# Level matmuls of a gated recurrence placed one unit later, with the operands of the first level made in the slot they have now

## The chip, the cores and the metric

One core of a Trainium2 chip runs the whole program. The metric is the device time of one execution in microseconds (us), as the median of several runs; lower is better. The engines of the core are TensorE (PE, matmuls), VectorE (DVE, elementwise work), ScalarE (ACT, functions and copies), GpSimd (POOL, elementwise work beside them) and SyncE (SP, which issues most transfers). Each works through its own queue in order and waits for the others by semaphores.

## The reference

A decoder layer over 512 tokens of width 1024. One input projection feeds three branches; the first of them is a gated linear recurrence with four heads of key and value width 128, and only its core bears on this change:

```python
def step(state, inp):
    qc, kc, vc, lc = inp
    b = jnp.cumsum(lc, axis=2)
    diff = b[:, :, :, None, :] - b[:, :, None, :, :]
    decay = jnp.where(causal, jnp.exp(jnp.where(causal, diff, 0.0)), 0.0)
    attn = jnp.einsum('bhtk,bhsk,bhtsk->bhts', qc, kc, decay)
    o = (jnp.einsum('bhts,bhsv->bhtv', attn, vc)
         + jnp.einsum('bhtk,bhkv->bhtv', qc * jnp.exp(b), state))
    b_last = b[:, :, -1:, :]
    new_state = (jnp.exp(b_last[:, :, 0, :])[..., None] * state
                 + jnp.einsum('bhsk,bhsv->bhkv', kc * jnp.exp(b_last - b), vc))
    return new_state, o
...
h = rms_norm(x, g_mix[l])
p = h @ w_in[l]
q, fp, iv, go, bg, cg, xc, u, v, gates = jnp.split(p, offsets, axis=-1)
o_a = hgrn2_mix(q, fp, iv, go, lbs[l], g_hgrn_out[l])
o_b = short_conv_mix(bg, cg, xc, w_conv[l])
o_c = spatial_gating_mix(u, v, sg_ln_g[l], sg_ln_b[l], w_sg[l], b_sg[l])
...
merged = jnp.sum(gate * y, axis=2)
x = x + merged @ w_o[l]
h2 = rms_norm(x, g_ffn[l])
x = x + jnp.square(jax.nn.relu(h2 @ w_ff1[l])) @ w_ff2[l]
```

A final RMS norm follows.

## The kernel before

The program is a list of **units**. A unit is one block of big matmuls on TensorE: typically a projection of 128 output columns for all 512 tokens, which is 24 matmuls of 128x512 (each product is made of three, L98 to L100, from a high and a low half of both operands). Units 0 to 3 project the forget gate, 4 to 7 the queries, 8 to 11 the values of the spatial branch, 12 to 15 its `u`, 16 to 19 the output gate, 20 to 31 the short convolution (`cg`, `xc`, `bg` in turn), and from 32 on come the merge gates and the branch outputs, then the output projection and the MLP.

Around each unit there are hooks, written into two tables by `at(...)`. What stands in `pre` for unit *i* (slot *i*) is recorded before the unit's matmuls, what stands in `post` behind them. Every engine keeps the recorded order, so a slot decides where in each engine's queue an instruction stands. Within a slot the order is: ScalarE's part of a weight split (`split_hi`, the high half `wh`), the evaluation of the unit before, the `take` hooks, VectorE's part of the weight split (`split_lo`, the low half `wl`), and then the other hooks in the order in which they were put down. A unit's weights are split two slots ahead of it.

The recurrence goes through seven levels. A level *l* builds the part of the causal attention matrix between neighbouring blocks of 2^l tokens. Heads are handled in two pairs, heads 0 and 1 (`p` = 0), and heads 2 and 3 (`p` = 1). For each pair and level there are three steps:
- `prep` (L281): ScalarE exponentials (L289, or L292 and L293), GpSimd additions that update the sums for the next level (L79, POOL), and VectorE multiplications that make the operands. At level 0 VectorE also does one reciprocal per head (L307), so that a head costs a reciprocal and four multiplications there.
- `level` (L318): four small matmuls per head (L326, 128x128) into a PSUM bank. The profile shows two records for each.
- `take` (L328): a predicated copy on VectorE (L332), which moves the wanted part of that bank into the attention tile and with that empties the bank.

Behind the levels come the states between the blocks of 128 tokens (`far_prep`, `far_turn`, `far_state` L362, `far_scan` L368 and L370), the outputs (`mix`, L379 and L381), a norm over the head (`mix_norm`, `mix_scale`) and a transpose (`head_turn`, L402, `head_out`). The constant `S0` is the slot at which the first level of the first pair is prepared; all other slots of the recurrence count from it. PSUM has eight banks, taken from one pool (`acc`, L72).

These lines set the slots:

```python
s0 = S0 + 2 * l + p
at(post, s0 + 1, level, pairs[p], l)
at(pre, s0 + 2, take, pairs[p], l)
at(pre, s0, prep, pairs[p], l)
```

Of the kernel before, what the change touches and what calls it, by code (L numbers as in the profile page):

```python
# [25 lines left out]
LB_FLOOR = 1e-30  # L26
LOG_SHIFT = 50
WARM = 8
S0 = 9
LN2 = 0.6931471805599453  # L30

V_GMIX, V_LB, V_GH, V_CONV, V_GFFN, V_GFIN, V_LG, V_LB2, V_N = 0, 8, 12, 16, 28, 36, 44, 48, 52
# [4 lines left out]
def trunk_kernel(ctx: ExitStack, tc, xT, x_t, w_f, w_t, w_bc, w_a, w_o, w_1, w_2, vecs, rows, gfin, w_sg, cst, lmask, out):  # L37
# [141 lines left out]
    pre, post = {}, {}  # L179

    def at(table, slot, fn, *a):
        table.setdefault(slot, []).append((fn, a))
# [397 lines left out]
    pairs = ((0, 1), (2, 3))  # L580
    for p in range(2):
        for l in range(7):
            s0 = S0 + 2 * l + p
            at(post, s0 + 1, level, pairs[p], l)
            at(pre, s0 + 2, take, pairs[p], l)
            at(pre, s0, prep, pairs[p], l)
        s0 = S0 + 14 + p
        at(pre, s0, far_prep, pairs[p])
        at(post, s0 + 1, far_turn, pairs[p])
        at(pre, s0 + 2, far_take, pairs[p])  # L590
        at(post, s0 + 2, far_state, pairs[p])
        at(pre, s0 + 3, far_scan, pairs[p])
        s0 += 3
        at(post, s0, mix, pairs[p])
        at(pre, s0 + 1, mix_norm, pairs[p])
        at(pre, s0 + 1, mix_scale, pairs[p])
        at(post, s0 + 2, head_turn, pairs[p])
        at(pre, s0 + 3, head_out, pairs[p])
# [569 lines left out]
```

## Time and profile before

| | |
|---|---|
| median of 3 runs | 835.8 us (835.66 to 835.86) |
| profiled execution, own time | 836.52 us |
| its span, first to last instruction | 834.7 us |
| PE busy | 819.6 us (98%) |
| DVE busy | 542.2 us (65%) |
| ACT busy | 346.0 us (41%) |
| POOL busy | 155.6 us (19%) |
| mean granted TensorE clock | 0.992 |

The profile is one execution. Busy times are shares of its span; time outside the span is start and end of the program. A busy TensorE can run at full clock (1.00, 2.4 GHz) or at half of it (1.2 GHz), which the granted clock shows as a mean over a stretch. Times in the rows below are us from the start of the span.

### The profile page before, as it was taken

To read this page: it belongs to the slowest core of one execution; us is meant where nothing else is said; L and a number is where in the kernel's file an instruction comes from. 1 tells how busy PE (TensorE), PEld (TensorE's weight loads), DVE (VectorE), ACT (ScalarE), POOL (GpSimd) and SP (SyncE) were. 2 spreads that over 40 slices of the span, in tenths; PEclk is the share of its full clock that TensorE was granted. 3 is DMA by queue.
4 is the path that set the end of the run, shared out by engine and by line. 5 is a ranking of instruction groups with operands and counts; after the bars stand their busy time and mean duration, and the time that the engine had idled before them with its cause. 6 is when DMAs were issued, how large, how long until landed. Compare 5 with 4: busy or idle time off the path is not lost.

```text
span 834.7 us, 9871 instructions
## 1 busy us (share of the span) xinstructions
PE 819.6 (98%) x3798; PEld 683.8 (82%) x3798; DVE 542.2 (65%) x706; ACT 346.0 (41%) x519; POOL 155.6 (19%) x187
## 2 busy tenths in 40 slices
PE   8999899999999999999999999999999999999995
PEld 7888688888988888888888888888888888888884
DVE  7556989878574455444554435868677777777763
ACT  7567365454433233222322434543434343434432
POOL 4312654562111000000000011202020202020000
PEclk9999899999999999999999999999999999999998
DMA  8322221212122322223235236657484838383502
GB/s 306 126 80 73 76 90 67 72 51 89 64 76 89 113 89 89 90 100 114 89 102 213 86 121 197 197 132 209 119 217 112 225 102 245 88 248 86 166 0 102
DMA packets 30431, 102.45 MB, mean 123 GB/s; under 512 B 3504, under 2 KB 3888, under 8 KB 30384
## 3 DMA queue, kind: packets, MB, share of 16 engines
q1 hardware_dynamic: 20736, 67.45, 23.3%
q0 software_dynamic: 9360, 34.08, 16.6%
q8 instruction: 30, 0.49, 0.2%
q10 hardware_dynamic: 288, 0.29, 0.1%
q14 instruction: 17, 0.14, 0.0%
HBM read 99.71 MB, written 2.10 MB: 122 GB/s over the span
## 4 chain that ended last, share of the span: by engine, by line
PE 95%; DVE 2%; issue 2%; DMA 1%; ACT 0%; SPq 0%; POOLq 0%; POOL 0%; DVEq 0%
PE acc L98 29%; PE acc L99 29%; PE acc L100 29%; PE acc L326 3%; PE acc L1058 1%; DVE h L79 1%; DVE wl L79 1%; DMA raw<-w_t 1%; PE acc L478 0%; PE acc L379 0%; PE acc L641 0%; DVE h L307 0%; PE acc L381 0%; PE acc L362 0%; PE acc L402 0%
## 5 line engine op out<-in xcount | busy, mean ns | idle before, releaser
L98 PE MATMUL acc<-x,wh 128*128 128x512 f32 x672 | 263.6, 392 | 0.0
L100 PE MATMUL acc<-x,wl 128*128 128x512 f32 x672 | 261.6, 389 | 0.0
L99 PE MATMUL acc<-x,wh 128*128 128x512 f32 x672 | 261.5, 389 | 0.0
L972 ACT ACTIVATE wh<-raw 128x1024 fp32r<-128x1024 f32 (+1 forms) x114 | 116.6, 1025 | 246.7 <-PE acc L99 143.5
L79 DVE TENSOR_TENSOR wl<-raw,wh 128x1024 fp32r<-128x1024 f32 (+1 forms) x120 | 153.2, 1278 | 44.1 <-ACT wh L972 43.8
L100 PEld LDWEIGHTS acc<-x,wl 128*128 128x128 f32 x672 | 126.1, 188 | 26.4
L98 PEld LDWEIGHTS acc<-x,wh 128*128 128x128 f32 x672 | 126.2, 188 | 25.8 <-issue 0.2
L99 PEld LDWEIGHTS acc<-x,wh 128*128 128x128 f32 x672 | 126.2, 188 | 25.7 <-issue 0.2
L79 DVE TENSOR_TENSOR h<-h,acc 128x512 f32<-128x512 f32 x118 | 75.6, 681 | 11.1 <-PE acc L100 11.0
L79 DVE TENSOR_TENSOR z<-z,z 128x1024 fp32r<-128x1024 f32 x51 | 61.6, 1218 | 32.1 <-ACT z L766 32.1
L692 ACT ACTIVATE h<-tmp 128x512 f32<-128x512 f32 x32 | 20.2, 633 | 125.6 <-DVE tmp L691 125.6
L766 ACT ACTIVATE z<-z 128x1024 fp32r<-128x1024 f32 x51 | 53.1, 1051 | 45.0 <-PE acc L100 28.2
L99 PE MATMUL acc<-z,h 128*128 128x512 f32 x184 | 71.6, 389 | 0.0
L100 PE MATMUL acc<-z,h 128*128 128x512 f32 x184 | 71.6, 389 | 0.0
L98 PE MATMUL acc<-z,h 128*128 128x512 f32 x184 | 71.6, 389 | 0.0
L79 DVE TENSOR_TENSOR h<-h,h 128x256 f32<-128x256 f32 (+4 forms) x89 | 66.4, 750 | 7.6 <-ACT h L745 3.6
L79 DVE TENSOR_TENSOR tmp<-acc,rb 128x512 f32<-128x512 f32 x28 | 19.3, 691 | 79.0 <-PE acc L100 79.0
L762 POOL DMA_DIRECT2D z<-w x28 | 24.5, 873 | 231.7 <-DVE z L79 195.6
L79 POOL TENSOR_TENSOR tmp<-tmp,tmp 128x512 f32<-128x512 f32 x15 | 20.0, 1332 | 198.0 <-DVE tmp L79 185.0
L691 DVE SCALAR_TENSOR_TENSOR tmp<-acc,rb 128x512 f32<-128x512 f32 x32 | 22.0, 686 | 30.9 <-PE acc L100 30.9
L100 PEld LDWEIGHTS acc<-z,h 128*128 128x128 f32 x184 | 34.5, 188 | 7.3
L98 PEld LDWEIGHTS acc<-z,h 128*128 128x128 f32 x184 | 34.5, 188 | 7.2
(187 smaller groups left out, 1071.7 us busy)
## 6 DMA issues: line engine op xcount, KB each, us to landing
z<-w POOLq DMA_DIRECT2D x65, 512.0 KB, 6.3
raw<-w_f SPq DMA_DIRECT2D x52, 512.0 KB, 3.3
raw<-w SPq DMA_DIRECT2D x34, 512.0 KB, 5.2
raw<-w_bc SPq DMA_DIRECT2D x8, 512.0 KB, 3.3
raw<-w_o SPq DMA_DIRECT2D x8, 512.0 KB, 3.3
raw<-w_t SPq DMA_DIRECT2D x4, 512.0 KB, 3.2
raw<-w_a SPq DMA_DIRECT2D x8, 256.0 KB, 2.6
h<-x_t SPq DMA_DIRECT2D x4, 512.0 KB, 7.0
```

The lines of the kernel that those rows point to most:

```text
L79: return e.tensor_tensor(out=o, in0=a, in1=b, op=op)
L98: pe.matmul(o, lh, rh, start=start, stop=False, skip_group_check=more)
L99: pe.matmul(o, lh, rl, start=False, stop=False, skip_group_check=more)
L100: pe.matmul(o, ll, rh, start=False, stop=stop, skip_group_check=more)
L326: pe.matmul(ps[:, cs(b)], kl[:, cs(b)], qk[:, cs(b)], start=True, stop=True)
L691: dve.scalar_tensor_tensor(out=t, in0=part["f", i], scalar=0.0, in1=part["r2b"], op0=ALU.max, op1=ALU.mult)
L692: act.activation(hf["a" if r < 2 else "b"][:, cs(r % 2, S)], t, AF.Square)
L762: pool.dma_start(wr[n, g], w_2[g, src[0], src[1]], accum_op=ALU.add)
L766: act.activation(hi, wr[src, g], AF.Copy)
L972: act.activation(hi[:, :n], raws[i][:, :n], AF.Copy)
L1058: pe.matmul(a4[t], lh, rh, start=j == 0 and rnd == 0, stop=j == KD - 1 and rnd == 2)
```

## The change

`S0` goes from 9 to 10, which puts every step of the recurrence one slot later, and the first level's `prep` alone is held at the slot that it has now.

```diff
@@ -26,7 +26,7 @@
 LOG_SHIFT = 50
 WARM = 8
-S0 = 9
+S0 = 10
 LN2 = 0.6931471805599453
@@ -583,7 +583,7 @@
             s0 = S0 + 2 * l + p
             at(post, s0 + 1, level, pairs[p], l)
             at(pre, s0 + 2, take, pairs[p], l)
-            at(pre, s0, prep, pairs[p], l)
+            at(pre, s0 - (l == 0), prep, pairs[p], l)
```

On TensorE, at the end of unit 10, the kernel before has level 0 of heads 0 and 1 (`acc_844` and `acc_849` are their banks, `h_394` and `h_395` head 0's operands, `h_434` and `h_435` head 1's) ahead of unit 11 (weights `wh_752`, `wl_753`).

```order
L100 MATMUL acc_727<-wh_705,x_243 128x512
L326 MATMUL acc_844<-h_394,h_395 128x128 x4
L326 MATMUL acc_849<-h_434,h_435 128x128 x4
L98 MATMUL acc_724<-wh_752,x_263 128x512
L99 MATMUL acc_724<-wl_753,x_263 128x512
```

In the changed kernel the same two rows stand behind unit 11 and ahead of unit 12 (`wh_798`, `wl_799`).

```order
L98 MATMUL acc_727<-wh_752,x_292 128x512
L99 MATMUL acc_727<-wl_753,x_292 128x512
L100 MATMUL acc_727<-wh_752,x_293 128x512
L326 MATMUL acc_874<-h_394,h_395 128x128 x4
L326 MATMUL acc_879<-h_434,h_435 128x128 x4
L98 MATMUL acc_910<-x_141,wh_798 128x512
```

The matmuls of one level have moved past the 24 of one unit. A unit later, in the changed kernel, level 0 of heads 2 and 3 (`h_474` to `h_516`) stands behind unit 12, and unit 13 (`wh_844`) follows; the waits are shown here.

```order
L326 MATMUL acc_935<-h_474,h_475 128x128 [waits DVE_49]
L326 MATMUL acc_935<-h_474,h_475 128x128 x3
L326 MATMUL acc_940<-h_515,h_516 128x128 [waits DVE_49,Activation_49]
L326 MATMUL acc_940<-h_515,h_516 128x128 x3
L98 MATMUL acc_967<-x_141,wh_844 128x512 [waits DVE_49]
```

The wait of unit 13's first matmul for VectorE (`DVE_49`) is, in the built program, for the predicated copy of `acc_874`, whose bank it takes over; in the kernel before it is unit 12 that waits for the copy of `acc_844`.

On VectorE, behind the operands of head 3 (`h_515`, `h_516`), the difference is this; `wl_845` is the low half of unit 13's weights, `wl_855` the same tile in the kernel before, and `wl_885` that of unit 14.

```order
 L79 TENSOR_TENSOR h_516<-z_514,h_515 128x256 x2
-L332 COPY_PREDICATED h_397<-lm,acc_844 128x512
-L332 COPY_PREDICATED h_437<-lm,acc_849 128x512
-L79 TENSOR_TENSOR wl_855<-raw_772,wh_854 128x1024
+L79 TENSOR_TENSOR wl_845<-raw_772,wh_844 128x1024
+L332 COPY_PREDICATED h_397<-lm,acc_874 128x512
+L332 COPY_PREDICATED h_437<-lm,acc_879 128x512
+L79 TENSOR_TENSOR wl_885<-raw_818,wh_884 128x1024
 L79 TENSOR_TENSOR h_395<-h_394,z_393 128x128x2
```

The two copies of level 0 now stand behind one weight split, and the operands of level 1 behind two. All VectorE rows ahead of these keep their order.

On ScalarE the exponentials of level 1 of heads 0 and 1 stand in the kernel before directly behind `wh_854`; in the changed kernel a further weight split and the four copies of unit 11's evaluation (L426) stand in front of them.

```order
L972 ACTIVATE wh_884<-raw_818 128x1024
L426 ACTIVATE z_887<-acc_724,rstd 128x512
L426 ACTIVATE z_887<-acc_725,rstd 128x512
L426 ACTIVATE z_890<-acc_726,rstd 128x512
L426 ACTIVATE z_890<-acc_727,rstd 128x512
L292 ACTIVATE h_394<-h_396 128x128x2
L293 ACTIVATE h_394<-z_393 128x128x2
```

GpSimd's additions of level 1 wait for these exponentials; their own order does not change there.

## Rows read from the trace of the kernel before

**Rows 1.** The page's busy times: engine, us, share of the span, instructions.

```profile
PE 819.6 (98%) x3798; PEld 683.8 (82%) x3798; DVE 542.2 (65%) x706; ACT 346.0 (41%) x519; POOL 155.6 (19%) x187
```

**Rows 2.** Waits of TensorE: total us, times, longest us.

```profile
PE acc L326 <- DVE h L79: 3.8, 2, 2.8
```

**Rows 3.** Stretches: us, busy PE, PEld, DVE, ACT, POOL, PEclk, DMA share, GB/s.

```profile
88.39:91.73 3.34, 2.48 (x11) 1.71 (x10) 3.34 (x6) 0.82 (x1) 3.18 (x5) 1.00 0.32 128
90.90:97.90 7.00, 3.21 (x17) 3.04 (x18) 7.00 (x9) 2.55 (x5) 5.18 (x7) 0.71 0.00 0
112.00:819.00 707.00, 707.00 (x3302) 591.43 (x3302) 459.52 (x593) 274.62 (x404) 114.73 (x139) 1.00 0.41 122
```

**Rows 4.** TensorE's timeline at level 0: start, duration, instruction, [idle before].

```profile
90.49 0.39 PE L100 MATMUL acc<-wh,x 128*128 128x512 f32 x1
91.86 1.16 PE L326 MATMUL acc<-h,h 128*128 128x128 f32 x8 [0.99 <-DVE h L79]
95.85 2.05 PE L326 MATMUL acc<-h,h 128*128 128x128 f32 x8 [2.83 <-DVE h L79]
```

**Rows 5.** Chain of work that ended last: start, us on the chain.

```profile
97.90 0.43 PE acc L98
...
100.86 0.23 PE acc L99
...
104.75 1.78 PE acc L326 x16
...
111.99 1.78 PE acc L326 x16
```

**Rows 6.** VectorE's timeline from 88 to 103 us.

```profile
88.39 1.67 DVE L79 TENSOR_TENSOR h<-h,h 128x256 f32<-128x256 f32 x2
...
91.73 1.74 DVE L307 RECIPROCAL h<-h 128x256 f32<-128x256 f32 x1
93.39 1.64 DVE L79 TENSOR_TENSOR h<-h,h 128x256 f32<-128x256 f32 x2
...
95.63 1.21 DVE L79 TENSOR_TENSOR wl<-raw,wh 128x1024 fp32r<-128x1024 f32 x1
96.76 1.74 DVE L307 RECIPROCAL h<-h 128x256 f32<-128x256 f32 x1
98.43 0.68 DVE L79 TENSOR_TENSOR h<-h,h 128x256 f32<-128x256 f32 x2
...
99.70 1.74 DVE L307 RECIPROCAL h<-h 128x256 f32<-128x256 f32 x1
...
102.64 1.34 DVE L332 COPY_PREDICATED h<-lm,acc 128x512 f32<-128x512 uint8 x2
```

**Rows 7.** GpSimd's timeline, additions of level 1, heads 0 and 1.

```profile
93.17 0.84 POOL L79 TENSOR_TENSOR h<-h,z 128x256 f32<-128x256 f32 x1
...
96.34 1.20 POOL L79 TENSOR_TENSOR h<-h,z 128x256 f32<-128x256 f32 x1 [1.59 <-ACT h L292]
97.62 0.61 POOL L79 TENSOR_TENSOR z<-z 128x256 f32<-128x256 f32 x1
```

**Rows 8.** ScalarE's timeline, level 1 behind unit 11's end.

```profile
108.03 0.45 ACT L292 ACTIVATE h<-h 128x256 f32<-128x256 f32 x1
```

**Rows 9.** Timelines of VectorE and TensorE at the outputs, 215 to 234 us.

```profile
215.92 1.05 PE L379 MATMUL acc<-z,h 128*128 128x128 f32 x8
...
225.84 1.05 PE L379 MATMUL acc<-z,h 128*128 128x128 f32 x8
226.73 0.83 PE L381 MATMUL acc<-h 128*128 128x128 f32 x6
...
222.31 0.28 DVE L368 COPY h<-acc 128x128 f32<-128x128 f32 x1
...
223.28 0.28 DVE L368 COPY h<-acc 128x128 f32<-128x128 f32 x1
...
233.53 0.69 DVE L79 TENSOR_TENSOR h<-acc,rr 128x512 f32<-128x512 f32 x1 [0.28 <-POOL tmp L499]
```

## The prediction before the run

> **What bounds the kernel now.** I read the table of busy times first: TensorE is busy for 98% of the span [rows 1], so a change pays only where TensorE stands still or runs at a lower clock. The list of who waited for whom comes next: TensorE's largest entry, 3.8 us, is at L326, the small matmuls of the recurrence, for VectorE [rows 2]. The table of stretches shows that this is one place: from 90.9 to 97.9 us TensorE is busy for 3.21 of 7.00 us while VectorE never rests, the granted clock is 0.71 there; from 112 to 819 us TensorE is busy for all of the 707 us at a clock of 1.00 [rows 3]. So this place is priced below, and behind it every microsecond that TensorE gains stays gained until the end of the program, unless the change makes a new wait.
>
> TensorE's own timeline shows the stop itself [rows 4]. Unit 10's last matmul starts at 90.49 us and lasts 0.39, so it ends at 90.88. Level 0 of the first pair (heads 0 and 1) stands next, and VectorE makes its operands with a reciprocal and four multiplications per head. Head 0's matmuls start at 91.86, head 1's only at 95.85. The chain that ended last goes on from there: head 1's eight records take 2.05 us, and the seven matmuls of unit 11 behind them are 0.43 us apart at first, where 0.23 is the step from 100.86 on [rows 5]. 0.43 against 0.23 is TensorE's lower level, 1.2 GHz, against 2.4; the fall came behind 0.98 us and then 2.83 us without a matmul.
>
> **The price of the stop.** Undisturbed, a unit with one pair's level takes 7.24 us: the chain shows level matmuls from 104.75 and, a unit later, from 111.99 [rows 5]. Their sixteen records take 1.78, so a unit is 5.46. From 90.88 to 111.99 TensorE does two units and two levels, 21.11 us where 2 x 7.24 = 14.48 would do: **6.63 us too much**. Its parts: 0.98 before head 0; 0.27 in head 0's records (1.16 for half of a 1.78 level); 2.83 before head 1; 1.16 in head 1's records (2.05 against 0.89); 1.37 in seven matmuls (97.90 to 100.86, 2.96 against 7 x 0.227). That is 6.61.
>
> **What the change removes and moves.** No instruction is added or dropped. Level 0 of the first pair goes behind unit 11, that of the second behind unit 12, while VectorE makes the operands in the same order as now, up to the second pair's last multiplication. In TensorE's new schedule, by ends: unit 10 at 90.88, unit 11 at 96.34, level 0 of pair 0 at 98.12, unit 12 at 103.58, level 0 of pair 1 at 105.36. What each step needs:
> - Unit 11 needs its low weight half, which VectorE makes ahead of head 0's multiplications at 88.39 [rows 6]. No wait.
> - Level 0 of pair 0 at 96.34 needs head 1's last multiplication, which now ends as the next weight split starts, at 95.63 [rows 6]. No wait, 0.7 us spare.
> - Unit 12 at 98.12 needs that weight split, which ends at 96.84. No wait.
> - Level 0 of pair 1 at 103.58 needs heads 2 and 3, whose last multiplication ends now at about 102.7, where the first predicated copy starts [rows 6]. No wait by the rows as they stand; head 3 is wanted only 0.89 later.
> - Unit 13 at about 105.1 (a unit's first matmul starts some 0.2 before the chain lets the level end) is the **new tight place**. Its first matmul waits for VectorE: the PSUM bank that it gets is that of head 0's level 0, and the predicated copy that empties it now stands behind heads 2 and 3 and one weight split more, and behind it on VectorE wait the second copy and level 1's operands.
>
> Its cost is bounded from both sides. ScalarE comes to the exponentials of level 1 of pair 0 one unit later, behind a weight split and four copies: behind the same work the second pair's now begin at 108.03 [rows 8], 3.28 after unit 11's end at 104.75 [rows 5], so these begin 3.28 after 96.34, at 99.6. GpSimd's additions at 93.17 and 96.34 [rows 7] are released by these and move to about 100.1 to 103. That relieves head 1, whose four multiplications took 2.24 us (93.39 to 95.63) where head 2's took 1.27 (98.43 to 99.70) with GpSimd idle from 98.23 on: everything from 95.63 on comes 0.97 earlier. In its place head 3 may be held up. Head 0's four took 3.34 (88.39 to 91.73) [rows 6], with GpSimd busy nearly throughout [rows 3]. So from 93.39: head 1 1.27, split 1.13, reciprocal 1.67, head 2 1.27, reciprocal 1.67: 100.40. Head 3 takes between 1.27 and 3.34, the next split 1.13, the first copy 0.7 (two overlapped take 1.34): the bank is free between **103.5 and 105.6**, against 105.1, and some 0.1 us more passes until TensorE runs. The wait is 0 to 0.6 us. Four additions stand against four multiplications, and the first of them starts during the reciprocal, so I go nearer to head 0's row: **0.3 us**.
>
> The Trainium skill, "SBUF — State Buffer", section "Who interferes with whom", says that a VectorE instruction with two SBUF inputs and a GpSimd instruction that reads SBUF exclude each other, and whichever starts first holds the port for its whole length. The trace agrees: 3.34 against 1.27 for the same four multiplications. By that rule each could wait out a whole addition, which as an estimate from the 0.61 us of GpSimd's shorter additions would be 2.4 us in all, a wait of 0.9 and 830.1 us; by the row it is 2.07 at most, a wait of 0.6 and 829.8 us.
>
> **Later places.** The whole recurrence behind level 0 comes one unit later, beside other convolution work. Per slot VectorE does the same operations, and level 1's operands follow the copies by a split and four short multiplications, with a whole unit before TensorE wants them. The tightest is the second pair's scan (L368, L370). Its slot now has the convolution step with three VectorE operations and a GpSimd product instead of one, in front of the first pair's scaling. The same chain exists now one slot later: from TensorE's 225.84 to the second scaling's end, 233.53 + 0.69, 8.4 us. Behind it head 2's part of the scan takes 0.97 (222.31 to 223.28 now), so its state is ready 9.4 us after the slot starts. TensorE wants it 10.8 us after (215.92 to 226.73) [rows 9]. That leaves 1.4 us: cost nothing.
>
> **Sum.** -6.63 + 0.3 = -6.3 us. The durations are of the profiled execution, whose own time, 836.5, is 0.7 over the median of the runs; its span of 834.7 would become 828.4. From the median: 835.8 - 6.3 = **829.5 us**.
>
> **Rivals.**
> 1. *The stop goes, with a short wait at unit 13* (forecast): 0 to 0.6 us of wait, 829.2 to 829.8; with some error in the steps 828.9 to 830.1. For it: all ready times above lie ahead of TensorE but one. Chance 0.77.
> 2. *The wait at unit 13 brings the low clock back.* If GpSimd holds up as much as head 0's row shows, TensorE stands for 0.6 us, and if the clock then falls as it did behind the stop of now, seven matmuls cost 1.4 more and the level behind them up to another 1: gain 3.6 to 4.6, 831.2 to 832.2. For it: head 0's row. Against it: one wait of 0.6 us is much shorter than the two behind which the clock fell here. Chance 0.13.
> 3. *Nothing changes:* VectorE is busy without a break from 90.90 to 97.90 [rows 3], and if its queue were the bound, the same wait would move to a later level: 835.8. That needs the bank at unit 13 some 6 us later than the upper bound. The order shows that the level does move. Chance 0.04.
> 4. *Slower:* the second pair's scan comes late behind the convolution and the scaling. It decides beyond 1.4 + 6.3 = 7.7 us of delay, and to be slower by over 0.2% it needs 9.4: 837.5 or more. The rows give no delay at all. Chance 0.03.
> The remaining 0.03 is a larger gain, to 828.6, should the parts of the stop be undercounted.
>
> About 0.2% (1.7 us) is what a measurement of this kernel can tell from no change. Cases 1, 2 and the larger gain are all faster by more than that: 0.92 with a little taken off for what I overlook; same 0.05; slower 0.03. The range takes in case 1 whole and the nearer part of case 2: 828.7 to 831.4.
>
> **What would show it.** Right: L326 disappears from TensorE's waits, or stays below 0.3 us; granted clock 1.00 from 90.9 on; level 0 of pair 0 starts near 96.2, of pair 1 near 103.4; a gap of 0 to 0.6 us before the first matmul of unit 13, ended by the predicated copy (L332); TensorE ahead by about 6.3 us at every later place. Wrong: a clock below 1.00 between 103 and 110 (case 2), a wait at L326 of over 1 us (case 3), a wait at L381 near 222 us (case 4).

## The result, and the profile after

| | before | change |
|---|---|---|
| median | 835.83 us (835.24 to 836.05, 6 runs) | 829.75 us (829.05 to 830.40, 6 runs) |
| ratio to before, 95% interval | | 0.9928 [0.9915, 0.9941] |
| profiled execution, own time | 836.52 us | 829.05 us |
| its span | 834.7 us | 827.3 us |
| mean granted TensorE clock | 0.992 | 0.997 |

The change makes the kernel 6.08 us faster between the medians. The forecast was 829.5 us.

The two profiled executions can't be subtracted as they stand. The program's first part takes a different time from run to run: the first record of L135, long before the recurrence, starts at 26.19 us in the trace of before and at 24.77 in that of the change. Unit 10's last matmul, shown here from the change, starts at 90.49 before and at 89.07 after, so it ends at 90.88 and at 89.46:

```profile
89.07 0.39 PE L100 MATMUL acc<-wh,x 128*128 128x512 f32 x1
```

So the times of after below are 1.42 us early against those of before, and gains are counted from the end of unit 10.

The page's busy times of the changed kernel answer to [rows 1]:

```profile
span 827.3 us, 9867 instructions
PE 816.8 (99%) x3798; PEld 682.6 (83%) x3798; DVE 543.8 (66%) x706; ACT 346.0 (42%) x519; POOL 156.2 (19%) x187
```

The counts of instructions are the same on every engine. TensorE's busy time has fallen by 2.8 us; VectorE's has not fallen, it is 1.6 us longer. The waits of TensorE (total, times, longest, in us) answer to [rows 2]; this is the whole list:

```profile
PE acc L989 <- DVE ones L982: 1.1, 1, 1.1
PE acc L98 <- DVE h L332: 0.3, 1, 0.3
```

L326 with its 3.8 us is gone. The first row is from the start of the program, and the list of before has it too, with the same 1.1 us. That list also has three waits of 1.2 us in all at L1058, ahead of L135; these belong to the different first part, not to the change. The second row is new, and it is the wait that the prediction named: a unit's first matmul waits for the predicated copy that empties its bank. The stretches (columns as in [rows 3]) show where the low clock was and is not any more:

```profile
90.90:97.90 7.00, 7.00 (x41) 6.09 (x40) 7.00 (x12) 2.97 (x5) 0.83 (x2) 1.00 0.24 75
...
101.00:105.00 4.00, 3.73 (x26) 3.21 (x25) 4.00 (x6) 2.38 (x5) 2.48 (x5) 1.00 0.14 33
105.00:110.00 5.00, 5.00 (x24) 4.15 (x23) 5.00 (x8) 0.25 (x1) 2.44 (x2) 1.00 0.56 187
```

The seventh number is the granted clock: 1.00 throughout, where 90.90 to 97.90 had 0.71. TensorE (the second number) is busy for all of the first stretch, where it was busy for 3.21 of 7.00. From there to 110 us it stands still for 0.27 us in all, between 101 and 105. VectorE (the fourth number) is still busy without a break: it was not made faster, TensorE only comes later. TensorE's timeline at the three levels and at unit 13's start answers to [rows 4]:

```profile
94.73 1.95 PE L326 MATMUL acc<-h,h 128*128 128x128 f32 x16
96.44 0.48 PE L98 MATMUL acc<-x,wh 128*128 128x512 f32 x1
...
101.97 1.95 PE L326 MATMUL acc<-h,h 128*128 128x128 f32 x16
104.19 0.50 PE L98 MATMUL acc<-x,wh 128*128 128x512 f32 x1 [0.27 <-DVE h L332]
...
109.78 1.95 PE L326 MATMUL acc<-h 128*128 128x128 f32 x16
```

Level 0 of each pair is now one run of sixteen records without a break. From the first to the second it takes 7.24 us, which is the undisturbed unit with a level of [rows 5]. From the second to the third it takes 7.81: unit 13 costs **0.57 us** too much, and its wait is the place. The chain of work that ended last passes through that place:

```profile
103.47 0.67 DVE h L332
104.14 0.04 issue
104.19 0.50 PE acc L98
...
109.94 1.78 PE acc L326 x16
```

VectorE's timeline says why the copy is late (it answers to [rows 6]), and GpSimd's, in the fence behind it, what stood beside it (to [rows 7]):

```profile
91.98 0.68 DVE L79 TENSOR_TENSOR h<-h,h 128x256 f32<-128x256 f32 x2
92.59 0.74 DVE L79 TENSOR_TENSOR h<-z,h 128x256 f32<-128x256 f32 x2
93.26 1.21 DVE L79 TENSOR_TENSOR wl<-raw,wh 128x1024 fp32r<-128x1024 f32 x1
...
99.00 1.60 DVE L79 TENSOR_TENSOR h<-h,h 128x256 f32<-128x256 f32 x2
100.52 1.84 DVE L79 TENSOR_TENSOR h<-z,h 128x256 f32<-128x256 f32 x2
102.26 1.21 DVE L79 TENSOR_TENSOR wl<-raw,wh 128x1024 fp32r<-128x1024 f32 x1
103.40 1.36 DVE L332 COPY_PREDICATED h<-lm,acc 128x512 f32<-128x512 uint8 x2
```

```profile
98.69 0.86 POOL L79 TENSOR_TENSOR h<-h,z 128x256 f32<-128x256 f32 x1 [6.89 <-ACT h L292]
99.64 0.68 POOL L79 TENSOR_TENSOR z<-z 128x256 f32<-128x256 f32 x1
100.28 1.03 POOL L79 TENSOR_TENSOR h<-h,z 128x256 f32<-128x256 f32 x1
101.38 0.67 POOL L79 TENSOR_TENSOR z<-z 128x256 f32<-128x256 f32 x1
```

Head 1's four multiplications (91.98 to 93.26) take 1.28 us with GpSimd idle, where they took 2.24. Head 3's four (99.00 to 102.26) take 3.26. In the kernel before they took 1.28, from the row below to the copy at 102.64:

```profile
101.36 0.69 DVE L79 TENSOR_TENSOR h<-h,h 128x256 f32<-128x256 f32 x2
```

So the additions of level 1 have left head 1 and come upon head 3. At the outputs, TensorE's timeline and then VectorE's answer to [rows 9]:

```profile
224.68 0.83 PE L381 MATMUL acc<-h 128*128 128x128 f32 x6
```

```profile
223.15 0.28 DVE L368 COPY h<-acc 128x128 f32<-128x128 f32 x1
```

Head 2's state of the scan is done when head 3's copy begins, at 223.15, and TensorE wants it at 224.68: 1.5 us to spare, 1.4 were reckoned.

**The account.** Before, TensorE took 6.63 us too much from unit 10's end to level 1. After, from 89.46 to level 1 at 109.94 on the chain, it does unit 11, level 0, unit 12, level 0 and unit 13, that is three units of 5.46 and two levels of 1.78, 19.94 us, and takes 20.48: 0.54 too much, which is unit 13's 0.57 but for the rounding of the steps. The difference, 6.09 us, accounts for the 6.08 by which the medians differ. That they agree so closely is luck: by the interval the gain is 4.9 to 7.1 us.

### The profile page after: what moved, and what is told of

It is laid out like the page before. It is cut to its first block, busy times and chain, and to the rows that moved or that the text cites. A ratio compares the mean times of both kernels' runs of the same rounds, so it can differ in the third digit from the quotient of the medians.

```text
span 827.3 us, 9867 instructions
## 1 busy us (share of the span) xinstructions
PE 816.8 (99%) x3798; PEld 682.6 (83%) x3798; DVE 543.8 (66%) x706; ACT 346.0 (42%) x519; POOL 156.2 (19%) x187
## 4 chain that ended last, share of the span: by engine, by line
PE 91%; DVE 4%; ACT 3%; issue 1%; POOLq 0%; POOL 0%; DVEq 0%; ACTq 0%
PE acc L98 28%; PE acc L100 28%; PE acc L99 28%; PE acc L1058 3%; PE acc L326 3%; DVE h L79 1%; DVE wl L79 1%; DVE h L307 1%; ACT h L257 1%; DVE h L270 0%; ACT wh L972 0%; PE acc L989 0%; ACT h L261 0%; PE acc L478 0%; PE acc L379 0%
```

## The experiments

Each kernel was run beside the kernel before on the same chip. The median of before there is 835.2 us in both groups of runs (23 runs beside the first four kernels, 14 beside the last four). Ratios are to it, with the 95% interval.

### Without the hold: the first level's operands move too

Does the change need the hold of `prep`, that is, the lead that it gives VectorE, or only the later matmuls? Against the change:

```diff
-            at(pre, s0 - (l == 0), prep, pairs[p], l)
+            at(pre, s0, prep, pairs[p], l)
```

> S0 = 10 without the hold: the first level's operands are made one slot later too, so the whole recurrence moves by one slot. Theory (VectorE's full queue makes TensorE stop, and the change gives it a unit more): VectorE now starts heads 0 and 1 only behind a third weight split, some 1.5 us later than before, head 1 is ready 0 to 1.2 us after TensorE wants it and head 3 0 to 2 us after, so 829.5 to 832 us; a wait at L326 of 0 to 3 us in all. Rival A (the hold is what brings the gain, a plain shift moves the stop along): 835.8 and a wait of 3.8 us at L326. Rival B (the lead does not matter at all): 829.2, no wait.

Measured: 828.39 us (828.14 to 830.03, 5 runs), 0.9924 [0.9911, 0.9936]. TensorE's timeline at the three levels:

```profile
94.68 1.95 PE L326 MATMUL acc<-h,h 128*128 128x128 f32 x16
...
101.92 1.95 PE L326 MATMUL acc<-h,h 128*128 128x128 f32 x16
...
109.16 1.95 PE L326 MATMUL acc<-h 128*128 128x128 f32 x16
```

They stand 7.24 us apart, twice: nothing is lost, at unit 13 neither. So the hold isn't needed, and the theory, which had 829.5 us at best and up to 3 us of waits, was wrong. The slot moves VectorE's operands by one weight split only (head 0's reciprocal starts at 87.05 us instead of 85.31), and level 0 still finds them ready. Unit 13 has no wait for two reasons, which this run doesn't part: in the built program of this kernel it takes over a bank that ScalarE empties (L426), not one of level 0's, and VectorE's copies begin 0.9 us sooner than the 103.40 of the change. The weight split that stood in front of the copies there stands in front of head 0 here, and the multiplications meet the additions less (head 0's take 2.30 us instead of 3.35, head 3's, from 100.03 on, 2.47 instead of 3.26):

```profile
102.50 1.37 DVE L332 COPY_PREDICATED h<-lm,acc 128x512 f32<-128x512 uint8 x2
```

### Only the steps behind the levels later

Is there a hidden cost in the later places, the states and outputs that come one unit later? This moves them alone; the levels stay. Against before:

```diff
-        s0 = S0 + 14 + p
+        s0 = S0 + 15 + p
```

> The kernel before, with the levels where they were and only the states, outputs, norm and transposes behind them (far_prep to head_out) one slot later. Theory: nothing waits there before or after, so 835.8 within 0.5 us and TensorE's stop of 3.8 us at L326 stays. Rival (part of the change's 6 us comes from the new neighbours of the later steps): up to 6 us faster, 829.8 to 835. Rival on the other side (the second pair's scan comes late behind the convolution): a wait at L381 near 226 us and over 836.5.

Measured: 835.52 us (834.16 to 836.62, 11 runs), 1.0004 [0.9996, 1.0013], no difference. The largest wait of TensorE is that of [rows 2], to the digit:

```profile
PE acc L326 <- DVE h L79: 3.8, 2, 2.8
```

None is listed at L379 or L381. The later places cost nothing and bring nothing; the whole gain is from the levels.

### GpSimd's additions behind head 3

If GpSimd's additions hold up head 3, and through it the copy and unit 13, then moving them out of the way should take the new wait away and leave all else. In `prep` at level 1, for heads 0 and 1, they are put off and recorded one slot later, behind those of heads 2 and 3. Against the change:

```diff
+            if (l, pair) == (1, (0, 1)):
+                late.append((rf, at_, as_, rt_))
+                continue
             tt(pool, rf, rf, at_, ALU.add)
             tt(pool, as_, as_, rt_, ALU.add)
...
+    def late_sums():
+        for rf, at_, as_, rt_ in late:
+            tt(pool, rf, rf, at_, ALU.add)
+            tt(pool, as_, as_, rt_, ALU.add)
...
+    at(pre, S0 + 3, late_sums)
```

> The changed kernel, with GpSimd's four level-1 additions of heads 0 and 1 put behind those of heads 2 and 3 in GpSimd's queue. Theory (they hold up head 3's four multiplications, and so the copy that unit 13 waits for): the four take about 1.3 us again instead of 3.26, the copy ends some 1.9 us earlier, TensorE's wait for L332 is gone, and the time falls by 0.5 to 0.6 us to about 829.2; the low end of level 1's operands stays ahead of TensorE. Rival (VectorE is late there by its own work): the wait of 0.3 us stays and the time with it, 829.75.

Measured: 828.34 us (828.19 to 828.54, 5 runs), 0.992 [0.9907, 0.9933]. The waits of TensorE, the whole list, are of the program's start alone; in the second fence stand VectorE's rows from head 3 to the copies, in the third GpSimd's first addition of level 1, which is head 2's now, and the first of those that were put off:

```profile
PE acc L1000 <- DVE ones L993: 1.1, 1, 1.1
PE acc L1069 <- DVE wl L79: 0.3, 1, 0.3
```

```profile
98.91 0.68 DVE L79 TENSOR_TENSOR h<-h,h 128x256 f32<-128x256 f32 x2
99.52 0.74 DVE L79 TENSOR_TENSOR h<-z,h 128x256 f32<-128x256 f32 x2
100.19 1.21 DVE L79 TENSOR_TENSOR wl<-raw,wh 128x1024 fp32r<-128x1024 f32 x1
101.32 1.34 DVE L342 COPY_PREDICATED h<-lm,acc 128x512 f32<-128x512 uint8 x2
```

```profile
103.33 1.16 POOL L79 TENSOR_TENSOR h<-h,z 128x256 f32<-128x256 f32 x1 [11.61 <-ACT h L294]
...
106.96 1.04 POOL L79 TENSOR_TENSOR h<-h,z 128x256 f32<-128x256 f32 x1
```

Head 3's four multiplications take 1.28 us (98.91 to 100.19) instead of 3.26, the copies start 2 us sooner, and the wait at unit 13 is gone, though in the built program unit 13 still takes over the bank of head 0's level 0. This shows the cause of the 0.57 us. The intervals of the two ratios overlap, but the five runs (828.19 to 828.54) all lie below the twelve of the change (828.77 to 830.40 in its two measurements); the trace shows where the gain is.

### The operands earlier, the matmuls where they were

Is it VectorE's lead, in slots, that was too short before? This gives it one slot more and leaves the matmuls. Against before:

```diff
-            at(pre, s0, prep, pairs[p], l)
+            at(pre, s0 - (l == 0), prep, pairs[p], l)
```

> The kernel before with S0 = 9, and only the first level's operands one slot earlier: in slots, the same lead of operands over matmuls as in the change, but TensorE's steps stay where they were. Theory (VectorE's queue is full there, so an earlier place only swaps the operands with one weight split, 1.1 to 2 us): head 1 is ready at about 93.3 to 94 in place of 95.7, unit 11 then waits for its own weight split, and the time is 833.5 to 835.8. Rival (the number of slots between operands and matmuls is what counts): as fast as the change, 829.5 to 830.

Measured: 834.36 us (832.71 to 836.33, 12 runs), 0.9989 [0.9978, 1.0]. TensorE's timeline at level 0 of heads 0 and 1, and the stretch behind:

```profile
89.19 1.05 PE L326 MATMUL acc<-h,h 128*128 128x128 f32 x8
93.52 1.74 PE L326 MATMUL acc<-h,h 128*128 128x128 f32 x8 [3.27 <-DVE h L79]
```

```profile
93.50:97.00 3.50, 3.48 (x13) 3.11 (x14) 3.50 (x5) 0.76 (x2) 1.81 (x2) 0.55 0.43 140
```

Head 0 is ready in time, but head 1 is still 3.27 us late, and the clock falls behind that wait. A slot is a place in a queue that is full already: head 1's operands are done 3.9 us behind unit 10's end (89.35 here, 93.29 where the next split starts) instead of 4.75. Unit 11 didn't wait for its own weight split, as the expectation had it. So the same hold that goes with the change gives little or nothing alone: 0.9 us between the medians, and the interval reaches from 1.8 us to none. It is the unit of TensorE's work put in front that pays.

### The change once more

A second measurement of the change, beside the three kernels that follow.

> The change once more, on the chip that runs the three below, so that they can be compared with it: 6.1 us faster than the kernel before (0.9928), a wait of about 0.3 us for L332 before unit 13 and none at L326.

Measured: 829.25 us (828.77 to 830.37, 6 runs), 0.9926 [0.9914, 0.9938]. TensorE's wait of 0.3 us at unit 13, for VectorE's L332, stands there again. The second and the third level start at 102.40 and 110.22, 7.82 us apart: the same 0.6 us over 7.24.

### Less work on VectorE in the kernel before

If VectorE's queue made the stop, then taking the reciprocals out of it should shorten the stop without moving TensorE. ScalarE makes the same factor with a second exponential. Against before:

```diff
                 act.activation(e[:, :256], as_, AF.Exp, scale=0.5)
+                act.activation(e[:, 256:], as_, AF.Exp, scale=-0.5)
...
-                dve.reciprocal(e[:, 256:], e[:, :256])
```

> The kernel before, with VectorE's reciprocal of level 0 replaced by a second ScalarE exponential of the negated argument, which is the same value; all places as before. VectorE loses 1.67 us per head. Theory (the stop is VectorE's queue): head 0 is ready 1.7 us and head 1 2.2 to 4.2 us earlier, against waits of 0.98 and 2.83 us; the stop shrinks to 0 to 1.7 us and the time to between 829.2 and 833, with no step of the recurrence moved. Rival (the distance in slots between operands and matmuls decides): 835.8.

Measured: 831.71 us (830.40 to 833.63, 6 runs), 0.9956 [0.9942, 0.997]. TensorE's wait at L326, the stretch behind, and VectorE's rows of head 1:

```profile
PE acc L326 <- DVE h L79: 2.2, 1, 2.2
```

```profile
93.00:97.00 4.00, 4.00 (x15) 3.18 (x15) 4.00 (x6) 0.15 (x1) 3.15 (x3) 0.59 0.43 133
```

```profile
88.70 1.82 DVE L79 TENSOR_TENSOR h<-h,h 128x256 f32<-128x256 f32 x2
90.44 1.81 DVE L79 TENSOR_TENSOR h<-z,h 128x256 f32<-128x256 f32 x2
```

Two reciprocals of 1.67 us lay ahead of head 1, 3.3 us, but the wait only fell from 3.8 to 2.2, more than the 1.7 that the expectation allowed: counted from unit 10's end, head 1 is done 1.9 us sooner, where 2.2 to 4.2 were expected. Head 1's multiplications take 3.48 us (88.70 to 92.18) instead of 2.24: GpSimd got its additions done beside the reciprocals before, and now does them beside the multiplications. The queue theory stands, with this correction to its size.

### The same beside the change

> The change with the same replacement. Theory: VectorE comes to the predicated copy some 6 us earlier, the wait at unit 13 goes, 0.5 to 0.6 us below the change (about 829.2 where the change has 829.75). Rival (the second exponentials hold ScalarE up and a weight split with it): as slow as the change or slower, with a wait of TensorE for ScalarE's L972.

The edit is that of the kernel above, made to the change. Measured: 828.67 us (828.20 to 828.99, 5 runs), 0.9919 [0.9906, 0.9931]. TensorE's timeline at the second and third level, and VectorE's copies:

```profile
102.52 1.95 PE L326 MATMUL acc<-h,h 128*128 128x128 f32 x16
...
109.76 1.95 PE L326 MATMUL acc<-h 128*128 128x128 f32 x16
```

```profile
97.82 1.36 DVE L332 COPY_PREDICATED h<-lm,acc 128x512 f32<-128x512 uint8 x2
```

The levels are 7.24 us apart. With all four reciprocals gone from VectorE's queue the copies come some 6 us sooner than in the change, and head 3's multiplications are over before GpSimd's additions begin; the built program has unit 13 on the same bank as in the change, and it waits for nothing. That makes the 0.57 us VectorE's lateness by a second way.

### The stop filled with matmuls that nobody reads

How much of the stop is the low clock? Here TensorE fills the two waits with 4 and 12 matmuls into a bank that nothing reads; the rest is the kernel before.

```diff
+            if (l, pair) == (0, (0, 1)):
+                if h == 0:
+                    part["fill"] = acc()
+                for i in range(4 if h == 0 else 12):
+                    pe.matmul(part["fill"], xh[i % KD][:, :P], xl[i % KD], start=True, stop=True)
```

> The kernel before, with 4 extra matmuls of 128x512 on TensorE ahead of head 0's level 0 and 12 ahead of head 1's, into a bank that nobody reads (0.91 and 2.72 us, about as long as TensorE's two waits there); nothing else moves. Theory (2.8 of the 6.6 us are the low clock behind the stop): the clock stays at 1.00, unit 11's first seven matmuls come at 0.23 us, and the time falls by 2.2 to 2.8 us to 833.0 to 833.6 although TensorE does more. Rival (the slow records have another cause than the standing still): 835.8, or more by what the fillers cost.

Measured: 833.08 us (832.44 to 834.99, 10 runs), 0.9978 [0.9968, 0.9989]. The stretch that had the low clock, and TensorE's timeline from unit 10's end to the second pair's level:

```profile
93.00:97.00 4.00, 4.00 (x23) 3.21 (x22) 4.00 (x7) 0.78 (x2) 2.33 (x4) 1.00 0.00 0
```

```profile
90.81 1.07 PE L327 MATMUL acc<-x,x 128*128 128x512 f32 x4
92.06 1.13 PE L331 MATMUL acc<-h,h 128*128 128x128 f32 x8 [0.18 <-DVE h L79]
92.94 2.99 PE L327 MATMUL acc<-x,x 128*128 128x512 f32 x12
95.88 1.16 PE L331 MATMUL acc<-h,h 128*128 128x128 f32 x8
...
102.33 1.95 PE L331 MATMUL acc<-h,h 128*128 128x128 f32 x16
```

The clock stays at 1.00, and head 1's records take 1.16 us, where they took 2.05. Head 1 comes no sooner, so the waits are still there, filled. From unit 10's end (90.58 + 0.39 = 90.97) to the second pair's level it takes 11.36 us, where the kernel before takes 13.71 (90.88 to 104.59): 2.35 less, and 2.1 between the medians. So about a third of the stop's 6.63 us was the low clock and most of the rest was waiting.

## Why the prediction was right

**The price of the stop, 6.63 us.** Right for the execution that it was read from: the change removes the stop whole. It is not the same in every execution, though. In the kernel with only the late steps moved, the same waits cost 0.7 us less, because the clock fell later. Filled with matmuls that nobody reads, the stop loses 2.35 us, where the prediction has 2.53 in the two parts at the lower clock (1.16 and 1.37). Of the 1.16, 0.27 is not the clock: head 1's eight records take 1.16 us instead of 0.89 there too, at 1.00.

**The steps without a wait.** Unit 11, level 0 of the first pair, unit 12 and level 0 of the second pair have no wait in the list. The levels start at 94.73 and 101.97, 96.15 and 103.39 on the time axis of before; about 96.2 and 103.4 were expected. The closest was head 3: its operands are done at 102.26, and TensorE comes to them at about 102.86 (101.97 + 0.89).

**Unit 13.** The place, the releaser and the cause were right. Head 1's four multiplications took 1.28 us (1.27 was the step), head 3's 3.26, close to the upper bound of 3.34 from head 0's row, and the first copy ended at 104.14, 105.56 on the time axis of before, where the upper bound was 105.6. The one term that was mis-sized is the cost taken between those bounds, **0.3 us: it measured 0.57**, with 0 to 0.6 as its range. The list of waits shows only 0.27 of it, because it counts from the end of the level's last record, 103.92 (101.97 + 1.95). Without a wait, unit 13's first matmul would have started before that end, at 103.68, 1.71 behind the level as at unit 12 (94.73 to 96.44). It started at 104.19, 0.51 later, and the small remainder is in the next matmuls, of which a few come 0.23 to 0.24 apart where the others are 0.23. The Trainium skill, "SBUF — State Buffer", section "Who interferes with whom", says that a VectorE instruction with two inputs in SBUF contends with a GpSimd instruction that reads SBUF; the trace agrees (3.26 us beside the additions, 1.28 without them, in the kernel with the additions put off). Its estimate in the prediction, 0.9 us for the wait, was too high; the row's bound held.

**Later places.** Nothing, as expected: the kernel with these steps alone moved ran in the time of before, and 1.5 us are to spare at L381.

**The rivals.** The low clock behind unit 13's wait didn't come: 1.00 from 90.9 to 110 us, though GpSimd held head 3 up nearly as much as that rival supposed (3.26 us of 3.34). TensorE's first matmul was 0.51 us late and its listed wait 0.27; what a longer wait there would do, no run shows. That nothing changes is excluded by the ratio, and so is a slower kernel: L381 waits for nothing.

**The sum.** 6.63 - 0.57 = 6.06 us against 6.3 forecast; the medians differ by 6.08. The mechanism was right in each step, and the miss of 0.2 us is unit 13's term. That the total comes out so near is in part luck, since the stop's price varies by more than that between executions.

**What is left.** Three kernels have no loss at unit 13: the one without the hold, the one with the additions put off and the one with the second exponential. They run in 828.3 to 828.7 us, some 0.6 to 1.4 below the two medians of the change, whose traces show 0.6 to be had. The intervals of the ratios tell none of them from the change. The runs tell one: those with the additions put off all lie below all of the change; those of the other two overlap with it. The kernel without the hold needs only the new `S0`, and nothing here shows a use for the hold.

## What to carry to other kernels

When TensorE stops for another engine's queue, look whether independent matmuls of a later step can go in front of the waiting ones: here one unit of them was worth the wait and the low clock behind it, and more lead for VectorE alone was worth 0.9 us of 6.1, not clear of noise. Then follow the instructions that empty the PSUM banks, since these move back with the work, and look at which engine empties the bank that the next unit gets. When work is taken off VectorE, see whether GpSimd used that time: what it did then meets the next instructions with two inputs.

## What the runs showed of the hardware

- The clock fell behind a single wait of 2.19 us (granted 0.59 from 93 to 97 us in the kernel with the second exponential) and behind one of 3.27 (0.55), and not behind one of 0.27. Between 88 and 112 us no run has a single wait whose length lies between these. Behind the 2.19 the clock was not low at once: head 1's eight records took 1.13 us, as in the stop that was filled, and the first step of 0.43 us between two matmuls is the one from 93.90, 1.5 us after TensorE had gone on (92.40).
- When the clock falls varies with the waits unchanged: with the same waits of 0.99 and 2.83 us as before, the kernel with only the late steps moved had head 1's records in 1.13 us instead of 2.05, and 12.01 us from head 0's start to the second pair's level instead of 12.73. So the price of the same stop differed by 0.7 us between these two executions.
- The time up to the first record of L135 varies by over 1.6 us between executions of kernels that don't differ there (24.64 us in one trace, 26.28 in another). That is more than unit 13's cost, so such a cost is read from a common place in the traces, not from two spans.
